# Group sizes, queue order and three seams of a streaming encoder layer on one Trainium2 core

## The chip, the core and the metric

The kernel is one program on one core of a Trainium2 chip. The metric is the device time of one execution in microseconds, as the median of several executions. The engines are called as in the profile: PE is TensorE (matrix products), DVE VectorE, ACT ScalarE, POOL GpSimd, and SP is the engine that here only issues DMA transfers.

## The reference

One layer on 512 prompt frames and 64 sample frames (576 columns, written HT halves of 256 + 32), model width 2048, all in float32:

```python
mod = silu(c) @ w_ada + b_ada                       # 2048 -> 6 x 2048
sh1, sc1, g1, sh2, sc2, g2 = split(mod, 6)
h = rmsnorm(x, norm1) * (1 + sc1) + sh1
proj = h @ w_in                                     # 2048 -> 7200 columns: q, k, v, gates of two head groups
...                                                 # gated linear attention (A), gated delta rule (B), per 64-frame block
x = x + g1 * (concat(o_a, o_b) @ w_out)             # 2048 -> 2048
h = rmsnorm(x, norm2) * (1 + sc2) + sh2
gate, val = split(h @ w_up, 2)                      # 2048 -> 2 x 5632
x = x + g2 * ((silu(conv3(gate) + b) * val) @ w_down)
y = rmsnorm(x, final_norm)
```

## The kernel before

**Products in three parts.** To reach float32 accuracy, every operand is split into a rounded part and a difference: weights `raw` into `wh` (ACT, rounding copy) and `wl = raw - wh` (DVE), activations into `hh` and `hl` in the same way. `mm6` multiplies one 128-row block of weights with one block of activations in six matmuls: `hh·wh`, `hl·wh`, `hh·wl`, each for the two halves of the columns. An engine works through its queue in order, so what is written ahead of an instruction on its engine is also executed ahead of it.

**First stage (`head`).** The modulation must be known before the first product, and its weights (`w_ada`) are as large as the projection's own. So the 16 blocks of 128 rows of x are taken in groups, `GROUPS` (first block, number of blocks). For each group `modulation(g)` runs eight steps (four 128-row chunks of `w_ada` each, out of `hraw` tiles), four for the scale `s1`, then four for the shift `mod`. After each four, the rows are copied from PSUM (`rw`, L864), transposed back to columns on PE (`bank<-consts,rw`), summed (`msum`, L869) and put into `mod` (L1006). Then `make(k)` forms a block's `hh` and `hl` through `split_mod`: scale and shift into `tmp` (L666 on ACT or L668 on DVE), rounding to `hh` (L669, ACT), difference `hl` (L670, DVE). While a group's products run for six early column tiles of `w_in` (`EARLY`, as three pairs, weights split in `pair_split`, L985 and L986, and partial sums kept by `sum_early` in `acc`), the next group's modulation steps are taken between the products: `product` steps the generator as a share of the products done. A narrow set of columns (`nar`, `ps_nar`) goes along with the first pair.

**In-projections.** The rest of `w_in` follows, with the recurrences of both head groups as jobs that a planner places between the matmuls by the costs in a table (their recorded line is L1978 on DVE and ACT, L1990 and L1994 on PE).

**Output projection.** `load_o` brings the heads' outputs of group B from DRAM and splits them. For each of 16 column tiles m, `x_tile(m)` loads the tile of x into one of two `xr` buffers and transposes it on PE (L1990 `bank<-consts,xr`, L1429), `gemm` multiplies, and `residual` adds.

**Up-projection.** For each step (t, c), a tile of columns and one of its seven products, `up_product` issues the matmuls (L1630 to L1632). Behind the first product, `norm_end` sums the squares over the partitions on PE (L1543), takes the power -1/2 on POOL (L1546), spreads the result into a diagonal `dg` (L1548, DVE) and broadcasts it over the partitions with PE again (L1554). The down-projection and the final norm follow.

Of the kernel before, what the change touches and what calls it, by code (L numbers as in the profile page):

```python
# [8 lines left out]
F32 = mybir.dt.float32  # L9
# [90 lines left out]
class Kern:  # L100
# [545 lines left out]

    def gemm(self, ps, src, acts, order=None, tick=lambda: None):

        n, i = len(acts), 0
        for k0 in order or range(0, n, 8):  # L650
            k1 = min(n, k0 + 8)
            wh, wl = self.wtile(src(k0, k1))
# [7 lines left out]

    def split_mod(self, x, s, b, hh, hl, tmp, other=False):

        nc = self.nc
        for c, q in ((slice(0, HP), 0), (slice(HP, HT), 1)):
            if other:
                nc.scalar.activation(tmp[:, :, c], x[:, :, c], AF.Identity, bias=b[:, q:q + 1], scale=s[:, q:q + 1])  # L666
                continue
            nc.vector.tensor_scalar(tmp[:, :, c], x[:, :, c], s[:, q:q + 1], b[:, q:q + 1], op0=ALU.mult, op1=ALU.add)  # L668
        nc.scalar.activation(hh, tmp, AF.Copy)  # L669
        nc.vector.tensor_tensor(hl, tmp, hh.bitcast(F32), op=ALU.subtract)  # L670

# [76 lines left out]
    def head(self, pool):  # L748
# [96 lines left out]
        def modulation(g):  # L845
            (m0, nm), per = GROUPS[g], per_tile(g)
            w = nm * P
            for n in range(8 * g, 8 * g + 8):
                _, mi, k0 = todo[n]
                ada_ahead(n + 1)  # L850
                if k0 == 0:
                    ps = self.bank()
                for k in (2, 3, 0, 1):
                    with self.tc.issue_after(last) if k == 0 else nullcontext():
                        T.matmul(ps[32 * k:32 * k + 32, :w], cs[:, k0 + k], got[n][k // per][:, k % per], start=(k0 == 0), stop=(k0 == KD - 4))  # L855
# [8 lines left out]
                V.tensor_copy(rw[:, :w], ps[:, :w])  # L864
# [4 lines left out]
                V.tensor_reduce(m, pc.rearrange("p b (j q) -> p b q j", j=4)[:, :, 0:2], axis=mybir.AxisListType.X, op=ALU.add)  # L869
# [7 lines left out]
        def w_ahead(n):  # L877
            for j in range(len(raws), min(n, len(pairs))):
                g, e = pairs[j]
                raws[j] = self.pair_load([off + h * P for _, off, h in EARLY[e:e + 2]], *GROUPS[g]), GROUPS[g][1]  # L880

        first, summed = modulation(0), []
# [12 lines left out]
        for b in range(5):  # L895
            if b < 4:
                x_norm(b + 1)
            if b < 3:
                x_square(b + 2)
            x_turn(b, (lambda b=b: x_scale(b + 1)) if b < 4 else None)  # L900
            if b > 0:
                next(first)
            if b == 3:
                v_turn(1)
        for _ in first:
# [6 lines left out]
        accs = [pool.tile([P, 2, HT], F32, tag=f"acc{e}", bufs=1, name=f"acc{e}") for e in range(len(EARLY))]  # L912

        def make(k):
            hh, hl = self.htiles(k)
            tmp = pool.tile([P, 2, HT], F32, tag="tmp", bufs=2, name=self.name("tmp"))
            self.split_mod(xT[:, k], s1[:, k], self.mod[:, 0, k], hh, hl, tmp, k in (1, 3))
            self.h.append((hh, hl))

        for g, (m0, nm) in enumerate(GROUPS):  # L920
# [6 lines left out]
            def product(e, j, k):  # L927
                nonlocal done, stepped
                self.mm6(ps[j], w[j][0][:, k - m0], w[j][1][:, k - m0], self.h[k], k == m0, k == ks[-1])
                done += 1  # L930
                while stepped < 10 and stepped * (units - nm) < 10 * done:
                    next(mods, None)
                    stepped += 1

            for e in range(0, len(EARLY), 2):
                w = self.pair_split(*raws[3 * g + e // 2])
                ps = [self.pgt() for _ in range(2)]
# [41 lines left out]

    def pair_split(self, raw, n):  # L980
# [3 lines left out]
        with self.tc.high_priority(offset=AHEAD):  # L984
            nc.scalar.activation(hi, raw[:, :2 * w], AF.Copy)  # L985
            nc.vector.tensor_tensor(lo, raw[:, :2 * w], hi.bitcast(F32), op=ALU.subtract)  # L986
        return [[x[:, e * w:(e + 1) * w].rearrange("p (k n) -> p k n", k=n) for x in (hi, lo)] for e in range(2)]
# [95 lines left out]

    def narrow_split(self, pool, src):

# [3 lines left out]
        nc.scalar.activation(s[:, :, 0:32], r, AF.Copy)  # L1089
        nc.vector.tensor_tensor(s[:, :, 32:64], r, s[:, :, 0:32].bitcast(F32), op=ALU.subtract)  # L1090
        return s
# [443 lines left out]
    def norm_end(self):  # L1535
# [6 lines left out]
        for b in range(5):  # L1542
# [5 lines left out]
        V.tensor_tensor(dg[:w], self.c["ident"][:w, :w].unsqueeze(1).to_broadcast([w, 5, w]),  # L1548
                        rs[:w, :5].unsqueeze(2).to_broadcast([w, 5, w]), op=ALU.mult)
        rb = self.rb = self.sq  # L1550
        dv = dg.rearrange("p b t -> p (b t)")
# [143 lines left out]
    def up(self):  # L1695
# [7 lines left out]
        for n, (t, c) in enumerate(steps):  # L1703
# [7 lines left out]
            if n == 0:  # L1711
                self.norm_end()

# [150 lines left out]
def layer_kernel(tc, i, o):  # L1864
    nc = tc.nc
    with ExitStack() as ctx:
# [15 lines left out]
        with ExitStack() as early:  # L1882
            K.wp = pool(early, "wp", "right", bufs=3)
            with ExitStack() as right:
# [9 lines left out]
                with ExitStack() as st:  # L1894
# [177 lines left out]
```

## Time and profile before

| | us |
|---|---|
| median of 3 executions | 2871.62 (2870.5 to 2878.71) |
| the profiled execution | 2873.51 |
| its span | 2871.4 |
| PE busy | 2809.1 (98%) |
| DVE busy | 2101.3 (73%) |
| ACT busy | 1189.0 (41%) |
| mean granted PE clock | 0.991 |
| PE busy in the first 200 us | 174.74 |
| PE busy from 1300 to 2780 us | 1480.0 |

The times inside the program are of the profiled execution and count from the start of its span; its own time is 2.1 us longer than the span. A row of the timeline has the start, the duration, the engine, the line of the code and the tiles (output<-inputs), and in brackets the time for which the engine had been idle before it and what released it. The granted clock is 1.00 at full speed and 0.50 where the throttle halves it. A matmul's recorded duration holds its run through the array, so successive ones overlap in the rows.

### The profile page before, as it was taken

The numbers are of one execution on the slowest core, as the hardware profiler recorded it, in microseconds if no ns is written. First come the engines' busy times: TensorE is split into PE (matmuls) and PEld (weight loads), VectorE is DVE, ScalarE is ACT, GpSimd is POOL, SyncE is SP. The second block draws the span as 40 slices with busy tenths as digits, with TensorE's granted clock in tenths as the row PEclk, the third lists the DMA queues.
The fourth block names the chain that finished last, engine by engine and source line by source line (L and its number), as shares of the span: only waits on it lengthen the run. The fifth ranks groups of instructions, "written<-read, shape, count | busy, mean of one in ns | idle before, by whom it ended". The sixth has DMA issues, their size and how long they took to land.

```text
span 2871.4 us, 52164 instructions
## 1 busy us (share of the span) xinstructions
PE 2809.1 (98%) x21028; PEld 2728.9 (95%) x21028; DVE 2101.3 (73%) x3592; ACT 1189.0 (41%) x2037; POOL 185.4 (6%) x244
## 2 busy tenths in 40 slices
PE   7999999999999999999999999999999999999998
PEld 4699999999999989999999999999999999999997
DVE  3478787787877888578888888888888855555565
ACT  4145555464534442454444444444444412212123
POOL 0001000010000000000111111111111000000000
PEclk8999999999999999999999999999999999999999
DMA  9965454455554567633333333333333653333221
GB/s 295 298 201 169 134 147 138 142 155 146 168 147 132 159 179 207 177 106 97 108 112 106 104 101 108 107 112 106 106 101 109 197 174 102 111 105 114 82 82 67
DMA packets 539797, 395.55 MB, mean 138 GB/s; under 512 B 59913, under 2 KB 477956, under 8 KB 539556
## 3 DMA queue, kind: packets, MB, share of 16 engines
q1 hardware_dynamic: 532212, 390.54, 45.8%
q8 instruction: 166, 2.72, 0.4%
q10 hardware_dynamic: 7344, 1.67, 0.3%
q14 instruction: 75, 0.61, 0.1%
HBM read 356.47 MB, written 35.67 MB: 137 GB/s over the span
## 4 chain that ended last, share of the span: by engine, by line
PE 86%; DVE 5%; issue 3%; DMA 3%; ACT 2%; POOL 1%; SPq 0%; ACTq 0%; POOLq 0%; DVEq 0%
PE g L643 29%; PE g L645 14%; PE bank L1631 12%; PE bank L1630 12%; PE bank L1632 11%; PE bank L1994 4%; DVE acc L1978 2%; PE bank L1990 1%; PE bank L855 1%; DVE wl L1978 1%; DVE m L1954 1%; DMA m<-gd 1%; DMA d<-m 1%; ACT m L1954 0%; DVE m L1978 0%
## 5 line engine op out<-in xcount | busy, mean ns | idle before, releaser
L1631 PE MATMUL bank<-slot,wh 128*128 128x290 f32 x2464 | 737.9, 299 | 0.0
L1630 PE MATMUL bank<-slot,wh 128*128 128x290 f32 x2464 | 734.2, 298 | 0.0
L1632 PE MATMUL bank<-slot,wl 128*128 128x290 f32 x2464 | 729.5, 296 | 0.0
L643 PE MATMUL g<-slot,wh 128*128 128x288 f32 x3168 | 550.4, 295 | 0.2 <-DVE slot L1978 0.2
L643 PE MATMUL g<-hh,wh 128*128 128x288 f32 x2048 | 475.2, 313 | 8.3 <-ACT hh L669 3.3
L1632 PEld LDWEIGHTS bank<-slot,wl 128*128 128x128 f32 x2464 | 471.4, 191 | 0.0
L1631 PEld LDWEIGHTS bank<-slot,wh 128*128 128x128 f32 x2464 | 468.8, 190 | 0.1
L1630 PEld LDWEIGHTS bank<-slot,wh 128*128 128x128 f32 x2464 | 463.8, 188 | 0.1
L643 PEld LDWEIGHTS g<-slot,wh 128*128 128x128 f32 x3168 | 463.0, 188 | 0.7 <-DVE slot L1978 0.5
L1978 ACT ACTIVATE wh<-raw 128x1024 fp32r<-128x1024 f32 x215 | 227.5, 1058 | 550.1 <-PE g L643 529.1
L643 PE MATMUL g<-hl,wh 128*128 128x288 f32 x2048 | 443.7, 298 | 0.0
L645 PE MATMUL g<-hh,wl 128*128 128x288 f32 x2048 | 441.9, 297 | 0.5 <-DVE wl L986 0.5
L1978 DVE SCALAR_TENSOR_TENSOR slot<-g,mod,slot 128x512 f32<-128x512 f32 (+1 forms) x448 | 201.8, 492 | 259.6 <-PE g L645 258.8
L643 PEld LDWEIGHTS g<-hh,wh 128*128 128x128 f32 x2048 | 327.0, 191 | 31.0 <-issue 16.3
L645 PE MATMUL g<-slot,wl 128*128 128x288 f32 x1584 | 340.9, 294 | 0.0
L643 PEld LDWEIGHTS g<-hl,wh 128*128 128x128 f32 x2048 | 331.9, 190 | 6.3 <-issue 5.4
L645 PEld LDWEIGHTS g<-hh,wl 128*128 128x128 f32 x2048 | 330.9, 189 | 6.1 <-issue 5.2
L1978 DVE TENSOR_TENSOR wl<-raw,wh 128x1024 fp32r<-128x1024 f32 x215 | 261.9, 1218 | 50.3 <-ACT wh L1978 47.9
L1577 ACT ACTIVATE wh<-raw 128x1024 fp32r<-128x1024 f32 x176 | 186.1, 1058 | 225.4 <-PE bank L1631 198.4
L645 PEld LDWEIGHTS g<-slot,wl 128*128 128x128 f32 x1584 | 255.3, 188 | 0.0
L1578 DVE TENSOR_TENSOR wl<-raw,wh 128x1024 fp32r<-128x1024 f32 x176 | 215.4, 1224 | 53.8 <-ACT wh L1577 53.8
L1577 ACT ACTIVATE wh<-s 128x1024 fp32r<-128x1024 f32 x132 | 140.1, 1062 | 210.7 <-DVE s L1588 109.3
(319 smaller groups left out, 3228.4 us busy)
## 6 DMA issues: line engine op xcount, KB each, us to landing
raw<-in_w_up_dram SPq DMA_DIRECT2D x176, 512.0 KB
raw<-in_w_in_dram SPq DMA_DIRECT2D x100, 512.0 KB
raw<-in_w_down_dram SPq DMA_DIRECT2D x88, 512.0 KB
aw<-in_w_ada_dram SPq DMA_DIRECT2D x79, 512.0 KB
xr<-in_w_ada_dram SPq DMA_DIRECT2D x49, 512.0 KB
hraw<-in_w_ada_dram SPq DMA_DIRECT2D x40, 512.0 KB
raw<-in_w_out_dram SPq DMA_DIRECT2D x32, 512.0 KB
slot<-actd SPq DMA_DIRECT2D x44, 288.0 KB
```

Of the source, the lines that this page charges most:

```text
L643: T.matmul(ps[:, h if bank is None else bank, :n], wh, x[:, h, :n], start=f, stop=False)
L645: T.matmul(ps[:, h if bank is None else bank, :n], wl, ah[:, h, :n], start=False, stop=stop)
L855: T.matmul(ps[32 * k:32 * k + 32, :w], cs[:, k0 + k], got[n][k // per][:, k % per], start=(k0 == 0), stop=(k0 == KD - 4))
L1577: self.nc.scalar.activation(hi, src, AF.Copy)
L1578: self.nc.vector.tensor_tensor(lo, src, hi.bitcast(F32), op=ALU.subtract)
L1630: T.matmul(ps, wh[:, j], hi, start=(c < 3 and j == 0), stop=False, skip_group_check=True)
L1631: T.matmul(ps, wh[:, j], lo, start=False, stop=False, skip_group_check=True)
L1632: T.matmul(ps, wl[:, j], hi, start=False, stop=(j == NPAIR - 1), skip_group_check=True)
L1954: return f(*a, **kw)
L1978: return f(*a, **kw)
L1990: return self.engine.transpose(out, *a)
L1994: return self.engine.matmul(out, *a, **kw)
```

## The change

In the first stage the 16 blocks are cut into six groups (2, 2, 3, 4, 3, 2) where there were five (2, 3, 4, 4, 3). `split_mod` is divided: `scale_x` multiplies x as soon as the scale is known, `shift_x` adds the shift while it rounds to `hh` (ACT, with a bias) and forms `hl` with one instruction per part (DVE). The first group's weight differences and the narrow difference are ordered behind the last row of the modulation (`issue_after`). After the copy of the rows, the modulation yields twice, and with a mark (`WAIT`) at which `product` stops stepping, so that products stand between the copy and the transposes; up to twelve steps are counted where there were ten. The vectors' transposes (`late`) are taken from any group behind the first.

Before the output projection the first weight tile is loaded and split after the fourth of eight `load_o`, and `x_tile(0)` comes behind the first tile's product. In the up-projection `norm_end` becomes a generator that stops after `dg`; its broadcast follows the second product.

```diff
-GROUPS = ((0, 2), (2, 3), (5, 4), (9, 4), (13, 3))
+GROUPS = ((0, 2), (2, 2), (4, 3), (7, 4), (11, 3), (14, 2))
...
-    def split_mod(self, x, s, b, hh, hl, tmp, other=False):
+    def scale_x(self, x, s, tmp, other=False):
         for c, q in ((slice(0, HP), 0), (slice(HP, HT), 1)):
             if other:
-                nc.scalar.activation(tmp[:, :, c], x[:, :, c], AF.Identity, bias=b[:, q:q + 1], scale=s[:, q:q + 1])
-                continue
-            nc.vector.tensor_scalar(tmp[:, :, c], x[:, :, c], s[:, q:q + 1], b[:, q:q + 1], op0=ALU.mult, op1=ALU.add)
-        nc.scalar.activation(hh, tmp, AF.Copy)
-        nc.vector.tensor_tensor(hl, tmp, hh.bitcast(F32), op=ALU.subtract)
+                nc.scalar.activation(tmp[:, :, c], x[:, :, c], AF.Copy, scale=s[:, q:q + 1])
+            else:
+                nc.vector.tensor_scalar_mul(tmp[:, :, c], x[:, :, c], s[:, q:q + 1])
+
+    def shift_x(self, b, hh, hl, tmp):
+        for c, q in parts:
+            nc.scalar.activation(hh[:, :, c], tmp[:, :, c], AF.Identity, bias=b[:, q:q + 1])
+        rounded = nc.cur_bb.bb.instructions[-1]
+        for c, q in parts:
+            nc.vector.scalar_tensor_tensor(hl[:, :, c], tmp[:, :, c], b[:, q:q + 1], hh[:, :, c].bitcast(F32),
+                                           op0=ALU.add, op1=ALU.subtract)
...
                 V.tensor_copy(rw[:, :w], ps[:, :w])
                 if g > 0:
-                    yield
+                    yield WAIT
+                    yield WAIT
...
+        for k in range(2):
+            scale(k)
         for _ in first:
             pass
-        nar = self.narrow_split(pool, nar)
+        summed_all = last()
+        begun = [self.pair_split(*raws[0], (None, summed_all))]
+        nar = self.narrow_split(pool, nar, summed_all)
+        for k in range(2):
+            make(k)
+        w_ahead(3)
+        begun += [self.pair_split(*raws[n], (rounded[-1], last())) for n in (1, 2)]
...
-                while stepped < 10 and stepped * (units - nm) < 10 * done:
-                    next(mods, None)
+                while stepped < 12 and (stepped - 2) * (units - nm - 2) < 10 * done:
+                    r = next(mods, None)
                     stepped += 1
+                    if stepped == 7 and not end:
+                        for i in range(2):
+                            scale(m0 + nm + i)
+                    if r is WAIT:
+                        break
...
-                        if g == 1 and e == 2 and late:
+                        if g > 0 and e == 2 and late:
                             late.pop(0)()
...
             self.up_product(t, c)
             if n == 0:
-                self.norm_end()
+                norm = self.norm_end()
+            if n < 2:
+                next(norm, None)
...
-                    ob = [K.load_o(k, lambda k=k: K.htiles(k)) for k in range(8, 16)]
+                    w, ob = {}, []
+                    for k in range(8, 16):
+                        ob.append(K.load_o(k, lambda k=k: K.htiles(k)))
+                        if k == 11:
+                            w[0] = K.wtile(K.w_cols("w_out", 0, 8)(0, 8))
...
-                        K.x1.append(K.x_tile(m))
-                        K.gemm(ps, K.w_cols("w_out", m, 8), ob, tick=K.tick)
+                        if m > 0:
+                            K.x1.append(K.x_tile(m))
+                        K.gemm(ps, K.w_cols("w_out", m, 8), ob, tick=K.tick, w=w.get(m))
+                        if m == 0:
+                            K.x1.append(K.x_tile(m))
```

On DVE at the entry to group 0, before, from the sum of the shift's rows on (`rw` are the copied rows, `wl` weight differences, `tmp` the scaled and shifted block, `nar` the narrow difference):

```order
L869 TENSOR_REDUCE msum_512<-bank_509 128x4
L986 TENSOR_TENSOR wl_619<-raw_355,wh_618 128x512
L1006 TENSOR_TENSOR mod<-msum_512,cols 128x4
L668 TENSOR_SCALAR tmp_534<-xT,s_218,mod 128x2x256
L668 TENSOR_SCALAR tmp_534<-xT,s_218,mod 128x2x32
L986 TENSOR_TENSOR wl_694<-raw_358,wh_693 128x512
L670 TENSOR_TENSOR hl_533<-tmp_534,hh_532 128x576
```

and the same place now:

```order
L880 TENSOR_REDUCE msum_521<-bank_518 128x4
L1043 TENSOR_TENSOR mod<-msum_521,cols 128x4
L1023 TENSOR_TENSOR wl_525<-raw_253,wh_524 128x512
L1128 TENSOR_TENSOR nar_528<-hraw_256,nar_528 128x2x32
L678 SCALAR_TENSOR_TENSOR hl_533<-tmp_489,mod,hh_532 128x2x256
L678 SCALAR_TENSOR_TENSOR hl_533<-tmp_489,mod,hh_532 128x2x32
```

`mod` has moved ahead of the weight difference, the scaling has left this place (it stands ahead of the copy of the rows), and two weight differences have moved behind `hl`, one ahead of it.

On PE at the entry to the second group, before, from the last modulation step of the shift to the first product of the new group (`bank_712` takes the transposes, `hh_736` is the new group's first block, `bank_786` the modulation of the group after it):

```order
L855 MATMUL bank_638<-hraw_608,cs 32x384 x2
L855 MATMUL bank_638<-hraw_607,cs 32x384 x2
L1990 MATMUL bank_712<-consts_185,rw_690 128x128 x3
L855 MATMUL bank_786<-hraw_644,cs 32x512 x2
L855 MATMUL bank_786<-hraw_643,cs 32x512
L643 MATMUL g_774<-hh_736,wh_770 128x288 x2
```

and now (`hh_728` is the new group's first block):

```order
L865 MATMUL bank_621<-hraw_511,cs 32x256 x4
L643 MATMUL g_696<-hh_538,wh_548 128x288 x2
L643 MATMUL g_696<-hl_539,wh_548 128x288 x2
L645 MATMUL g_696<-hh_538,wl_549 128x288
L2038 MATMUL bank_683<-consts_185,rw_668 128x128 x2
...
L643 MATMUL g_697<-hl_539,wh_548 128x288 x2
L645 MATMUL g_697<-hh_538,wl_549 128x288 x2
L865 MATMUL bank_776<-hraw_581,cs 32x384 x2
L865 MATMUL bank_776<-hraw_580,cs 32x384
L643 MATMUL g_764<-hh_728,wh_760 128x288 x2
```

Five matmuls of the running group now stand between the modulation step and the transposes, and thirteen more (the one left of `g_696` and the twelve of `g_697`) between these and the next group's modulation.

On PE at the start of the output projection, before (`g_11956` is the first column tile, `xr_11958` the first tile of x):

```order
L645 MATMUL g_11735<-hh_1111,wl_11822 128x288 x2
L643 MATMUL g_11956<-hh_11910,wh_11972 128x288
L1990 MATMUL bank_11962<-consts_185,xr_11958 128x128 x4
L1429 MATMUL bank_11968<-consts_185,xr_11958 128x64
L643 MATMUL g_11956<-hh_11910,wh_11972 128x288
```

and now the end of that column tile (`g_12081`) and the start of the second (`g_12173`):

```order
L645 MATMUL g_12081<-hh_12077,wl_12053 128x288 x2
L2038 MATMUL bank_12162<-consts_185,xr_12158 128x128 x4
L1467 MATMUL bank_12168<-consts_185,xr_12158 128x64
L643 MATMUL g_12173<-hh_12029,wh_12189 128x288 x2
L643 MATMUL g_12173<-hl_12030,wh_12189 128x288 x2
L2038 MATMUL bank_12179<-consts_185,xr_12175 128x128 x4
```

The transposes of x's first tile have moved from the first matmul of the column tile to behind its last, and those of the second tile follow after four matmuls of the second column tile.

More of the change, by code (lines that the diff above doesn't have):

```diff
@@ L645, in mm6, with gemm @@
             T.matmul(ps[:, h if bank is None else bank, :n], wl, ah[:, h, :n], start=False, stop=stop)
-    def gemm(self, ps, src, acts, order=None, tick=lambda: None):
+    def gemm(self, ps, src, acts, order=None, tick=lambda: None, w=None):
         n, i = len(acts), 0
@@ L651, in gemm @@
             k1 = min(n, k0 + 8)
[L652 removed]
+            wh, wl = w or self.wtile(src(k0, k1))
             for k in range(k0, k1):
@@ L880, in w_ahead, with scale, make @@
                 raws[j] = self.pair_load([off + h * P for _, off, h in EARLY[e:e + 2]], *GROUPS[g]), GROUPS[g][1]
+        scaled, rounded = {}, []
+        def scale(k):
+            if k not in scaled:
+                tmp = scaled[k] = pool.tile([P, 2, HT], F32, tag="tmp", bufs=2, name=self.name("tmp"))
+                self.scale_x(xT[:, k], s1[:, k], tmp, k in (1, 3))
+        def make(k):
+            hh, hl = self.htiles(k)
+            scale(k)
+            rounded.append(self.shift_x(self.mod[:, 0, k], hh, hl, scaled[k]))
+            self.h.append((hh, hl))
         first, summed = modulation(0), []
@@ L978, in pair_load, with after, pair_split @@
         return raw
-    def pair_split(self, raw, n):
+    def after(self, ins):
+        return self.tc.issue_after(ins) if ins is not None else nullcontext()
+    def pair_split(self, raw, n, order=None):
         nc, w = self.nc, n * P
         hi, lo = [self.wq.tile([P, 1024], F32R, tag="w" + c, bufs=3, name=self.name("w" + c))[:, :2 * w] for c in "hl"]
-        with self.tc.high_priority(offset=AHEAD):
-            nc.scalar.activation(hi, raw[:, :2 * w], AF.Copy)
-            nc.vector.tensor_tensor(lo, raw[:, :2 * w], hi.bitcast(F32), op=ALU.subtract)
+        act, dve = order or (None, None)
+        with self.tc.high_priority(offset=AHEAD) if order is None else nullcontext():
+            with self.after(act):
+                nc.scalar.activation(hi, raw[:, :2 * w], AF.Copy)
+            with self.after(dve):
+                nc.vector.tensor_tensor(lo, raw[:, :2 * w], hi.bitcast(F32), op=ALU.subtract)
         return [[x[:, e * w:(e + 1) * w].rearrange("p (k n) -> p k n", k=n) for x in (hi, lo)] for e in range(2)]
@@ L1089, in narrow_split @@
         nc.scalar.activation(s[:, :, 0:32], r, AF.Copy)
-        nc.vector.tensor_tensor(s[:, :, 32:64], r, s[:, :, 0:32].bitcast(F32), op=ALU.subtract)
+        with self.after(dve):
+            nc.vector.tensor_tensor(s[:, :, 32:64], r, s[:, :, 0:32].bitcast(F32), op=ALU.subtract)
         return s
@@ L1549, in norm_end @@
                         rs[:w, :5].unsqueeze(2).to_broadcast([w, 5, w]), op=ALU.mult)
+        yield
         rb = self.rb = self.sq
```

13 lines of the change are left out of this document (6 added, 7 removed).

## The prediction

> **What bounds the kernel now.** I read the profile's page first, then the windows by stage, then the timeline around every stop of TensorE. The page:
>
> ```profile
> span 2871.4 us, 52164 instructions
> PE 2809.1 (98%) x21028; PEld 2728.9 (95%) x21028; DVE 2101.3 (73%) x3592; ACT 1189.0 (41%) x2037; POOL 185.4 (6%) x244
> ```
>
> TensorE is busy for 2809.1 of 2871.4 us, so all its stops together are 62 us; nothing in the change lessens the products themselves. The windows of the first and the longest stage (length; then busy time and count of each engine; then granted clock, DMA share, GB/s) say where the stops are:
>
> ```profile
> 0.00:200.00 200.00, 174.74 (x1225) 129.51 (x1226) 99.06 (x223) 67.86 (x121) 5.18 (x16) 0.95 0.85 268
> 1300.00:2780.00 1480.00, 1480.00 (x11047) 1480.00 (x11046) 1089.35 (x1451) 558.00 (x657) 106.70 (x131) 1.00 0.38 113
> ```
>
> The up-projection (last row) has no stop at all, at 1480 / 11047 = 0.134 us a matmul. What can be won lies in the first 200 us (25.3 us idle, clock 0.95) and at two seams, near 1045 and 1288, whose rows stand below. All the edits of the change lie there.
>
> **First stage, entry to group 0.** The turn from modulation rows to the first product, in the timeline (start, duration, instruction, and in brackets the idle time before it and its releaser):
>
> ```profile
> 38.34 0.44 PE L1990 MATMUL bank<-consts,rw 128*128 128x128 f32 x2 [0.56 <-DVE rw L864]
> 38.82 0.17 DVE L869 TENSOR_REDUCE msum<-bank 128x4 f32<-128x16 f32 x1 [0.54 <-PE bank L1990]
> 38.93 0.69 DVE L986 TENSOR_TENSOR wl<-raw,wh 128x512 fp32r<-128x512 f32 x1
> 39.54 0.16 DVE L1006 TENSOR_TENSOR mod<-msum,cols 128x4 f32<-128x4 f32 x1
> 39.79 0.81 ACT L666 ACTIVATE tmp<-xT,mod,s 128x512 f32<-128x512 f32 x1 [1.69 <-DVE mod L1006]
> 40.54 0.68 ACT L669 ACTIVATE hh<-tmp 128x576 fp32r<-128x576 f32 x1
> 41.36 0.72 PE L1097 MATMUL ps_nar<-hh,nar 128*66 128x288 f32 x2 [2.58 <-ACT hh L669]
> ```
>
> The chain is msum, a weight difference that isn't needed yet (0.69), mod, scale and shift, rounding to hh, product: 2.58 us of TensorE. The change puts mod directly behind msum (saves 0.6) and scales ahead of the chain, so that one shift of 0.7 to 0.9 (256-column halves of the 0.68 row, and a second start) stands where tmp 0.81 and hh 0.68 stood (saves 0.7 to 0.9). The first product moves from 41.36 to about 39.85: **-1.5**. The weight difference, the narrow difference and hl now stand behind mod, but six matmuls that need only hh (0.8 us at full clock) cover them.
>
> What the pause does to the clock:
>
> ```profile
> 37.35:40.76 3.41, 0.88 (x10) 0.20 (x2) 2.33 (x7) 1.60 (x3) 0.00 (x0) 1.00 1.03 374
> 46.00:48.00 2.00, 2.00 (x7) 1.03 (x6) 0.00 (x0) 0.00 (x0) 0.00 (x0) 0.60 0.35 129
> 64.66:68.07 3.41, 1.35 (x10) 0.28 (x8) 1.95 (x6) 1.79 (x4) 0.00 (x0) 1.00 1.05 407
> 70.00:72.00 2.00, 2.00 (x8) 1.32 (x8) 0.90 (x2) 0.86 (x2) 0.00 (x0) 0.63 0.35 86
> ```
>
> After a 3.41-us stretch with 0.88 us of matmuls the clock is halved until about 47.6; after one with 1.35 us, until about 71.5. The first costs half of some 6.2 busy us, 3.1; the second half of 3.4, 1.7. With the products starting at 39.85 the first stretch would hold 0.88 + 0.91 = 1.79 of its 3.41 us, 52%. The trace halves at 40% and, after the pause of 1.25 at 102 (below), not at 63%; 52% lies between. I take half: **-1.6**, between 0 and -3.1. The Trainium skill ("TensorE: Matmul & The Clock Gate", HAM oscillation) says to avoid PE-idle gaps longer than about 3.4 us. By that rule none of the stops named in this text would touch the clock, every clock term would be zero, and the sum would come to -6.4 instead of -13.5. This trace contradicts it: the gaps here are 2.58 and 2.06 us and the clock was 0.50. The same page's fixed windows of about 3.4 us (Part 1) agree with the 3.41 us between the changes in the rows.
>
> **First stage, entry to the next group.**
>
> ```profile
> 64.46 0.55 PE L1990 MATMUL bank<-consts,rw 128*128 128x128 f32 x3 [0.71 <-DVE rw L864]
> 65.15 0.96 DVE L986 TENSOR_TENSOR wl<-raw,wh 128x768 fp32r<-128x768 f32 x1
> 68.06 0.85 PE L643 MATMUL g<-hh,wh 128*128 128x288 f32 x2 [2.06 <-ACT hh L669]
> ```
>
> In the changed order the transposes stand behind 5 or more matmuls (0.67 us for the 0.71), and 13 matmuls and three modulation matmuls (about 2.0 us) stand between them and the first matmul that needs hh. The difference wl still precedes mod here, but is 512 instead of 768 columns wide, and the scaling is done early: msum to hh takes 0.17 + 0.69 + 0.16 + 0.7 and hand-overs, about 2.0. So 0.7 and 1.6 us of idle go, and the 1.7 us of half clock: **-4.0**. Late next is hl, 0.4 us behind hh, which I keep of the 2.06.
>
> The other waits of the stage that the edits touch:
>
> ```profile
> 80.00 0.44 PE L1990 MATMUL bank<-consts,rw 128*128 128x128 f32 x2 [0.84 <-DVE rw L864]
> 83.83 0.53 PE L645 MATMUL g<-hh,wl 128*128 128x288 f32 x2 [0.53 <-DVE wl L986]
> 90.06 0.29 PE L712 MATMUL bank<-consts,hs 88*128 88x88 f32 x1 [0.77 <-DVE cols L713]
> 90.70 0.28 PE L712 MATMUL bank<-consts,hs 72*128 72x72 f32 x1 [0.34 <-DVE cols L713]
> 102.05 0.80 PE L643 MATMUL g<-hh,wh 128*128 128x288 f32 x4 [1.25 <-ACT hh L669]
> 112.90 0.44 PE L1990 MATMUL bank<-consts,rw 128*128 128x128 f32 x2 [0.39 <-DVE rw L864]
> ```
>
> They come to 4.1. In the changed order four later turns still have their transposes directly behind the last modulation matmul, for which I carry 0.7 each (the 0.71 row), and 0.4 for a late hl: 3.2 stay, **-0.9**.
>
> What six groups cost more than five is eight modulation steps:
>
> ```profile
> 62.90 0.85 PE L855 MATMUL bank<-hraw,cs 128*32 128x384 f32 x8
> 73.20 1.07 PE L855 MATMUL bank<-hraw,cs 128*32 128x512 f32 x8
> ```
>
> The columns stay the same in all, so only the fixed part is new: 128 columns are 1.07 - 0.85 = 0.22 us, which leaves 0.85 - 3 x 0.22 = 0.19 a step, some of it the last matmul's drain. Eight are 1.0 to 1.5, and up to 2.6 if what follows a step starts late too: **+1.6**. The six more partial sums run on VectorE and ScalarE, which are busy 99 and 68 of the 200 us: nothing while that holds, 0.7 each where a product would wait. ScalarE gets one more table load in the chain of the narrow columns at the stage's end; the one below takes 1.28, and the waits there are partly ScalarE's: 0 to 1.3, **+0.6**. The two 2-block groups also bring the modulation weights' deadlines closer (rival 2); the rows there leave a few us, so **+1.0**, 0 to 7.6. The stage: -1.5 - 1.6 - 4.0 - 0.9 + 1.6 + 0.6 + 1.0 = **-4.8**.
>
> **Seam before the output projection.**
>
> ```profile
> 1040.19 1.05 SPq L739 DMA_DIRECT2D raw<-in_w_out_dram  x2
> 1042.43 1.28 ACT L1978 ACT_TABLE_LOAD   x1
> 1045.88 1.06 ACT L1978 ACTIVATE wh<-raw 128x1024 fp32r<-128x1024 f32 x1 [1.28 <-DMA raw<-in_w_out_dram]
> 1046.99 0.40 PE L643 MATMUL g<-hh,wh 128*128 128x288 f32 x1 [3.03 <-ACT wh L1978]
> 1048.65 1.09 PE L1990 MATMUL bank<-consts,xr 128*128 128x128 f32 x4 [1.25 <-DMA xr<-in_x_prompt_dram]
> 1050.00:1052.00 2.00, 2.00 (x11) 2.00 (x10) 2.00 (x5) 0.48 (x2) 0.00 (x0) 0.50 0.89 244
> 1054.00:1056.00 2.00, 2.00 (x16) 2.00 (x15) 0.00 (x0) 0.00 (x0) 0.00 (x0) 0.87 1.00 310
> ```
>
> The first weight tile is asked for at 1040.19 and rounded at 1046.9: 3.03 us of waiting, then 1.25 for x, then half clock until about 1054.5 over 5.8 busy us, 2.9: 7.2 lost. Now the weights are asked for eight SP transfers earlier and split before the seam; x's transposes stand behind the 48 matmuls of column tile 0 (6.4 us). What is late next is the second x tile: its transposes follow the first products of tile 1, and its buffer comes free only when the last rows have been split, which now stand behind more ScalarE and VectorE work. That gives 0 to 5 us of new wait; I carry 2.2: **-5.0**.
>
> **Seam after the first up-projection product.**
>
> ```profile
> 1286.00 1.08 PE L1543 MATMUL bank<-consts,sqa 128*116 128x1 f32 x10
> 1288.96 0.76 DVE L1548 TENSOR_TENSOR dg<-consts,s 116x580 f32<-116x580 f32 x1 [1.31 <-POOL s L1546]
> 1289.78 2.08 PE L1554 MATMUL bank<-dg,consts 116*128 116x290 f32 x4 [2.69 <-DVE dg L1548]
> 1290.00:1292.00 2.00, 2.00 (x6) 1.42 (x6) 2.00 (x5) 0.85 (x3) 0.00 (x0) 0.51 0.09 23
> ```
>
> 2.69 idle and half of about 3.4 us at half clock, 4.4. The yield puts 24 matmuls (24 x 0.134 = 3.2 us) into the gap. VectorE is full in the window of the last row, and the products now ask for their split tiles 4 us earlier, so I count half as given back: **-2.2** (-4.4 to 0).
>
> **Inside the in-projections** the planner's turns shift:
>
> ```profile
> 275.19 1.10 PE L1994 MATMUL bank<-m,m 128*128 128x64 f32 x8 [2.78 <-DVE m L1978]
> ```
>
> These squarings of the inverse stand some 11 matmuls (1.5 us) later in the changed order: **-1.5** (-3 to +1).
>
> **Sum.** -4.8 - 5.0 - 2.2 - 1.5 = -13.5. The profiled execution took 2873.5 (span 2871.4 and 2.1 around it), 1.9 above the median of 2871.6; carried to the median the forecast is **2858.1**.
>
> **Rivals.**
> 1. *The first stage gives nothing.* The clock still halves (+1.6), the steps cost their upper end (+1.0) and a fifth group entry brings another 1.25 besides the waits at 80 to 113 returning (+0.9 and 1.25): -4.8 becomes 0. For it: the chain mod, shift, hl is repeated once more. Then 2871.6 - 8.7 = 2862.9, or a little over.
> 2. *Transfers take over: slower.*
>
> ```profile
> 60.00:70.00 10.00, 7.23 (x44) 3.24 (x43) 4.44 (x10) 4.33 (x7) 0.00 (x0) 0.90 1.04 376
> 80.00:90.00 10.00, 8.76 (x62) 7.17 (x62) 3.47 (x9) 0.85 (x1) 0.32 (x1) 1.00 1.05 352
> ```
>
>    A block's modulation and early weights are 2.5 MB. With groups of 2, 2, 3, 4 blocks, 17.5 MB are wanted between about 44 us, when the tiles are full, and the end of the third group near 98: 324 GB/s. Full windows gave 352 and 376, which is enough. It decides the other way below 324: at the stage's mean of 268 the weights come 11.3 us late, in some five pauses of over 2 us that each halve the clock for a stretch (1.7 each, 8.5). With the seams' -8.7 and the stage's other terms at about +0.5 that is +11.6: 2883. Smaller rows per transfer speak for it, the 350s against.
> 3. *The wait at 1045 only moves* to the second x tile or weight tile: its bound of 5 us and no clock gained there leave -2: 2861.1.
>
> **Chances.** Forecast 0.54, rival 1 0.20, rival 3 0.11, rival 2 0.15. About 0.3% (8.6 us) is what a measurement of this kernel tells from no change, so faster is below 2863.0 and slower above 2880.2. Of the forecast 0.48 are faster and 0.06 same; of rival 1 0.06 and 0.14; of rival 3 0.06 and 0.05; of rival 2 0.02 are same and 0.13 slower. Faster 0.60, same 0.27, slower 0.13. The range starts at 2848 (clock kept throughout, no new wait at the seams: -1.6, -2.2, -2.2, -1.5 and 2.5 more) and reaches to 2875, over rivals 1 and 3; it leaves out rival 2 and some 3% below.
>
> **What would show it.** Right: the first narrow product near 39.9 with under 1.3 us idle ahead of it; no half clock around 70; no pause above 1 us at the weights of the output projection, and its clock full; 24 matmuls of the next product between the column sums and the broadcast. Wrong: TensorE waiting for hraw or raw between 60 and 100 at under 324 GB/s (rival 2); four or more pauses above 1 us at group entries (rival 1); a stop of over 3 us about 7 us into the output projection (rival 3).

## The result, and the profile after

The changed kernel takes 2854.29 us (median of 4 runs, 2851.53 to 2856.73) against 2871.26 before (four executions): a ratio of 0.9935 (95% interval 0.9916 to 0.9954), 17 us less by the medians and 18.7 by the ratio, which is not the quotient of the two medians. Run again beside the experiments below it took 2853.67 against 2871.84, ratio 0.9943 (0.9929 to 0.9957). The forecast was 2858.1 in a range of 2848 to 2875. Its profiled execution took 2851.53. The first part of its page, and the windows that answer to those of before:

```profile
span 2849.8 us, 52385 instructions
PE 2796.4 (98%) x21092; PEld 2724.1 (96%) x21092; DVE 2109.3 (74%) x3625; ACT 1193.3 (42%) x2058; POOL 186.5 (7%) x245
```

```profile
0.00:200.00 200.00, 178.18 (x1369) 140.52 (x1370) 114.15 (x274) 79.72 (x153) 5.29 (x17) 0.99 0.87 277
37.40:40.80 3.40, 3.40 (x16) 2.89 (x20) 2.69 (x6) 1.78 (x4) 0.00 (x0) 0.50 1.00 332
40.00:60.00 20.00, 20.00 (x163) 13.38 (x166) 4.77 (x15) 7.26 (x15) 0.26 (x1) 0.98 0.94 325
66.00:70.00 4.00, 2.28 (x17) 2.04 (x16) 2.38 (x9) 0.00 (x0) 0.32 (x1) 1.00 1.05 372
1040.00:1060.00 20.00, 20.00 (x141) 16.48 (x140) 13.11 (x27) 7.07 (x18) 2.51 (x2) 1.00 0.83 237
1264.00:1274.00 10.00, 8.84 (x64) 8.29 (x63) 8.27 (x18) 7.39 (x17) 1.50 (x3) 1.00 0.49 135
```

TensorE's busy time fell by 12.7 us although it does 64 matmul records more. Most of the reason stands in the view of spans and clocks, before and then after:

```profile
core 0: 2871.4 us, clock 0.991
```

```profile
core 0: 2849.8 us, clock 0.996
```

A ledger can be made of these rows. Clock lost: 0.009 x 2871.4 = 25.8 us before, 0.004 x 2849.8 = 11.4 after, so 14.4 less. Idle: 2871.4 - 2809.1 = 62.3 before, 53.4 after, 8.9 less. What is left is work at full clock, 1.7 more. Together 21.6, the difference of the spans. (The clocks are given to 0.001, so the first and the last term are good to some 2 us. They also count halved time in which TensorE stood idle, at the program's end above all: over its busy time the halved stretches cost 20.8 and 6.3 us, again 14.5 apart.) Two thirds of the gain of these two executions is clock, not idle time.

Not all of that is the change's. Up to the last transposes ahead of group 0 both kernels issue the same 148 matmuls, and the profile of the kernel before had two halved stretches there, with 9.7 us of busy time; its transposes came 2.9 us later. The rows are the kernel before, the kernel before with the norm seam alone, which has the same first stage, and the changed kernel:

```profile
0.00:38.34 38.34, 22.81 (x148) 13.61 (x148) 18.24 (x53) 23.79 (x58) 3.82 (x12) 0.87 0.96 292
0.00:35.80 35.80, 20.92 (x148) 13.11 (x148) 18.22 (x53) 22.50 (x57) 3.82 (x12) 1.00 0.96 288
0.00:35.44 35.44, 20.50 (x148) 12.99 (x149) 18.07 (x53) 23.10 (x58) 3.78 (x12) 1.00 0.97 288
```

So 4.9 of the 14.5 stand ahead of the change. Another 1.9 lie in the in-projections, which no edit touches directly. At the changed places the clock gave 7.8 us (9.5 before, 1.7 after) and idle time 7.9.

The timeline at the changed places. Entry to group 0:

```profile
35.92 0.17 DVE L880 TENSOR_REDUCE msum<-bank 128x4 f32<-128x16 f32 x1 [0.53 <-PE bank L2038]
36.12 0.16 DVE L1043 TENSOR_TENSOR mod<-msum,cols 128x4 f32<-128x4 f32 x1
36.23 0.69 DVE L1023 TENSOR_TENSOR wl<-raw,wh 128x512 fp32r<-128x512 f32 x1
36.32 1.81 ACT L675 ACTIVATE hh<-tmp,mod 128x512 fp32r<-128x512 f32 x4 [0.75 <-DVE mod L1043]
37.38 0.69 PE L1135 MATMUL ps_nar<-hh,nar 128*66 128x288 f32 x2 [1.50 <-ACT hh L675]
59.97 0.63 ACT L1021 ACTIVATE wh<-raw 128x512 fp32r<-128x512 f32 x1 [2.02 <-DMA raw<-in_w_in_dram]
66.72 1.21 DVE L668 TENSOR_SCALAR tmp<-xT,s 128x512 f32<-128x512 f32 x4
67.84 0.68 DVE L1023 TENSOR_TENSOR wl<-raw,wh 128x512 fp32r<-128x512 f32 x1
68.58 0.53 PE L645 MATMUL g<-hh,wl 128*128 128x288 f32 x2 [1.72 <-DVE wl L1023]
```

`mod` follows `msum` directly, and the pause is 1.50 us instead of 2.58; one half-clock stretch of 3.4 us follows (second window) where there were 6.8. At the second entry, near 55, TensorE does not stop at all (third window: 20.00 of 20.00). The last rows are a new wait, in the second group's second pair of column tiles. The difference `wl` is late, but not for a transfer: its `raw` and `wh` were there from 60.60 on. It stands in VectorE's queue behind the sum for the third group's scale (from 66.10) and behind the early scaling (1.21), which the change put there.

The seam of the output projection, the norm, and the squarings inside the in-projections:

```profile
1037.67 0.60 PE L2038 MATMUL bank<-consts,xr 128*128 128x128 f32 x4
1038.78 0.24 PE L1467 MATMUL bank<-consts,xr 64*128 64x64 f32 x1 [0.51 <-DMA xr<-in_x_sample_dram]
1265.80 1.18 PE L1581 MATMUL bank<-consts,sqa 128*116 128x1 f32 x10
1270.15 1.14 PE L1593 MATMUL bank<-dg,consts 116*128 116x290 f32 x4
1272.73 0.40 PE L1669 MATMUL bank<-slot,wh 128*128 128x290 f32 x1 [1.17 <-ACT sqa L1594]
266.90 1.10 PE L2042 MATMUL bank<-m,m 128*128 128x64 f32 x8 [1.56 <-DVE m L2026]
```

Of 3.03 + 1.25 us at the output projection 0.51 is left, and the clock stays at 1.00. The broadcast of the norm starts without a wait; the next product waits 1.17 for its copy by ScalarE. The squarings wait 1.56 instead of 2.78 in this execution, but 3.83 in another profile of the same kernel (shown below, with the in-projections).

### The profile page after: what moved, and what is told of

It reads as the page before. It is cut to its first block, busy times and chain, and to the rows that moved or that the text cites. A ratio compares the mean times of both kernels' runs of the same rounds, so it can differ in the third digit from the quotient of the medians.

```text
span 2849.8 us, 52385 instructions
## 1 busy us (share of the span) xinstructions
PE 2796.4 (98%) x21092; PEld 2724.1 (96%) x21092; DVE 2109.3 (74%) x3625; ACT 1193.3 (42%) x2058; POOL 186.5 (7%) x245
## 4 chain that ended last, share of the span: by engine, by line
PE 84%; DVE 7%; issue 3%; DMA 3%; ACT 2%; POOL 1%; SPq 0%; ACTq 0%; DVEq 0%; POOLq 0%
PE g L643 28%; PE g L645 14%; PE bank L1670 12%; PE bank L1669 11%; PE bank L1671 11%; PE bank L2042 4%; DVE acc L2026 2%; PE bank L2038 1%; PE bank L865 1%; DVE wl L2026 1%; DVE m L2002 1%; DMA d<-m 0%; DMA hs<-in_x_prompt_dram 0%; DVE ca L2026 0%; DMA cm<-d 0%
```

## The experiments

All are compared with the kernel before on the same chip. Three chips were used, one for each group of four that ran together; on these the kernel before took 2873.09 (the parts alone and five groups), 2870.34 (eight groups, the weights without x, both with matmuls that nothing reads) and 2871.84 us (six groups, the queue order, the plain yield and the changed kernel again). The differences in us are worked out from the ratios; the medians alone would give up to 3 us more or less.

**The parts alone.** *First stage only*: the change without the hunks of the two seams; two of them are shown.

```diff
-                norm = self.norm_end()
-            if n < 2:
-                next(norm, None)
+                self.norm_end()
...
-                        if k == 11:
-                            w[0] = K.wtile(K.w_cols("w_out", 0, 8)(0, 8))
```

> The change's first-stage edits alone, both seams as before. Theory A (each part works at its own place, read from the two traces: lead of the changed kernel at the start of the output projection 13.4 us, of which 2.9 stood there before the first edited instruction): about -9 against before, 2862 us, first product under 1.6 us of idle behind the transposes, no halved clock around 65 to 72. Theory B (the stage gives nothing because the extra group's steps and waits eat it, and the lead is a chance of the clock at the start): 0 to -2, 2870 us.

2864.23 us, ratio 0.9974 (0.9966 to 0.9983): -7.5 us. A, a little less than its -9, and with a pause of 1.50 at the entry. Its other sign failed: the clock was halved at 66.93, behind the new wait of 1.72 us, which left the clock whole in both profiles of the changed kernel.

```profile
66.93:70.34 3.41, 3.41 (x19) 3.13 (x21) 0.76 (x1) 0.07 (x1) 0.00 (x0) 0.50 1.12 355
```

*Output seam only*: the kernel before with the hunks of `gemm` and `w[0]`, and `x_tile(0)` behind the product.

> The output projection's seam alone in the kernel before: first weight tile loaded and split early, first x tile behind the first product. Theory A: the seam's 4.3 us of idle and 2.9 us of half clock go, all but 0.5: -6.5, 2865 us, no pause above 1 us and the clock at 1.00 in the 20 us around the seam. Theory B (the wait moves to the second x tile, whose buffer comes free later): -2, 2869 us, with a pause of 2 to 5 us about 7 us into the output projection.

2862.71 us, ratio 0.9972 (0.9962 to 0.9981): -8.0. A. The only pause there is 0.69, for x:

```profile
1047.90 0.24 PE L1429 MATMUL bank<-consts,xr 64*128 64x64 f32 x1 [0.69 <-DMA xr<-in_x_sample_dram]
```

*Norm seam only*: the kernel before with the `yield` behind `dg` and the second `next`.

> Only the norm's broadcast moved behind the second up-projection product, in the kernel before. Theory A: the 2.69 us pause and the half clock (1.7) go and about 1.2 to 2.2 come back as a wait on the broadcast's copy and on VectorE: -2, 2869 us. Theory B (VectorE is full there, all is given back): 0, 2871 us, with TensorE waits of 2 us or more between 1290 and 1310.

2868.86 us, ratio 0.9988 (0.9979 to 0.9996): -3.4, interval -6.0 to -1.1. A, with the rest of the wait where it is in the changed kernel:

```profile
1293.21 0.40 PE L1631 MATMUL bank<-slot,wh 128*128 128x290 f32 x1 [1.14 <-ACT sqa L1556]
```

The three parts add to -18.9; the whole measured -18.7 (0.9935) and -16.4 (0.9943). Each part is good to 2 or 3 us, so this agrees, but it doesn't prove that the parts are independent.

**The weights without x.** The kernel before with `w[0]`, but `x_tile(0)` ahead of the product as before.

```diff
+                        if k == 11:
+                            w[0] = K.wtile(K.w_cols("w_out", 0, 8)(0, 8))
...
                         K.x1.append(K.x_tile(m))
-                        K.gemm(ps, K.w_cols("w_out", m, 8), ob, tick=K.tick)
+                        K.gemm(ps, K.w_cols("w_out", m, 8), ob, tick=K.tick, w=w.get(m))
```

> The kernel before with the output projection's first weight tile early, but x's first tile still transposed ahead of the first product. Theory A (x's transfer, asked for at 1042 and landed at 1048.5, is the wait behind the wait: TensorE then stops some 4 us for x and the clock still halves): 0 to -1.5 against before, 2872 us. Theory B (the weights alone make the stop): -6, 2867 us.

2867.45 us, ratio 0.9982 (0.9972 to 0.9993): -5.2. My reading (A) was wrong: x's transfer, asked for at 1045.49, came within 3.7 us, where it had taken 6.3, probably because the two large weight transfers were out of its way. TensorE waited 0.69 for it, and the clock was not halved:

```profile
1049.16 0.63 PE L1994 MATMUL bank<-consts,xr 128*128 128x128 f32 x4 [0.69 <-DMA xr<-in_x_prompt_dram]
```

What moving x as well is worth is not settled: 3 us by the ratios, but the intervals of -5.2 and -8.0 overlap, and in both traces one wait of 0.69 for x is left.

**The group sizes.** The change with five groups, with eight, and the kernel before with six.

```diff
-GROUPS = ((0, 2), (2, 2), (4, 3), (7, 4), (11, 3), (14, 2))
+GROUPS = ((0, 2), (2, 3), (5, 4), (9, 4), (13, 3))
```

> The whole change but with the old five groups (2, 3, 4, 4, 3). Theory A (the sixth group costs its eight steps, 1.5 us, and one more entry of about 0.8, and what it saves is no more than that): 2852 to 2855 us, within 2 us of the changed kernel. Theory B (the short second group is what lets the entry at 54 to 58 us pass without a pause): a pause of 1.5 us or more and a halved clock come back at the second entry, 2857 us or more.

2858.16 us, ratio 0.9957 (0.9945 to 0.9969): -12.4. The mechanism of B is there, a pause at the second entry with a halved clock behind it. The transposes stand directly behind 16 modulation matmuls again and wait 0.71 (at 58.79), in spite of the marks:

```profile
61.56 0.67 PE L643 MATMUL g<-hh,wh 128*128 128x288 f32 x3 [2.23 <-ACT hh L675]
60.00:70.00 10.00, 8.44 (x41) 4.35 (x42) 3.83 (x10) 3.81 (x8) 0.00 (x0) 0.83 0.83 269
```

The intervals of five and six groups overlap, so the 4 us between them are likely, not settled. The seams alone gave -8.0 and -3.4; of -12.4 that leaves some -1 for all edits of the first stage but the sizes (an estimate from three ratios, good to 5 us or so).

```diff
+GROUPS = tuple((n, 2) for n in range(0, 16, 2))
```

> The whole change with eight groups of two blocks. Theory A (a group costs its eight modulation steps at 0.19 us fixed and one entry of about 0.8): two more groups than six are +3.0 + 1.6, 2858 to 2861 us. Theory B (short groups starve on transfers, the prediction's rival 2): pauses above 1.5 us at hraw or raw between 60 and 150 us, 2865 us or more. Theory C (all entries get cheap, a pause below the clock's limit each): 2854 us or less.

2856.04 us, ratio 0.9943 (0.9930 to 0.9955): the same as six groups within the measurement. B is refuted: no pause at hraw or raw. A is not borne out either: 16 more steps, but behind the entry to group 0 no pause above 0.69 us up to 200 us and no halved clock. That is the mechanism of C, 2 us above its bound:

```profile
36.00:200.00 164.00, 156.99 (x1351) 130.79 (x1352) 105.37 (x252) 56.85 (x106) 1.72 (x7) 1.00 0.86 272
152.17 0.53 PE L643 MATMUL g<-hh,wh 128*128 128x288 f32 x2 [0.69 <-ACT wh L1021]
```

In the kernel before, six groups need one more edit, since the vectors' turns no longer fit into the second group:

```diff
+GROUPS = ((0, 2), (2, 2), (4, 3), (7, 4), (11, 3), (14, 2))
...
-                        if g == 1 and e == 2 and late:
+                        if g > 0 and e == 2 and late:
```

> The kernel before with the six groups alone (and the vectors' turns taken from any later group), scaling, queue order and yields as before. Theory A (small groups help only where the entry is short): the 2.6 and 2.1 us pauses with their halved clock stay, eight more steps: +1 to +2, 2873 us. Theory B (the group sizes alone carry the stage's gain): -3 to -5, 2867 us.

2865.90 us, ratio 0.9986 (0.9977 to 0.9995): -4.0, so B. The modulation's smaller tiles arrive early enough that a step of the next group now runs inside the entry pause, and cuts it into 1.05 and 0.89. At the second entry the old code now has its transposes among products, without a wait (third row), and neither the 0.71 nor the 2.06 of before comes back:

```profile
36.18 0.63 PE L855 MATMUL bank<-hraw,cs 128*32 128x256 f32 x6 [1.05 <-DMA hraw<-in_w_ada_dram]
37.70 0.45 PE L1097 MATMUL ps_nar<-hh,nar 128*66 128x288 f32 x2 [0.89 <-ACT hh L669]
52.23 0.38 PE L1990 MATMUL bank<-consts,rw 128*128 128x128 f32 x2
36.00:80.00 44.00, 39.95 (x311) 26.71 (x312) 18.48 (x44) 12.47 (x21) 0.58 (x2) 1.00 0.96 326
```

**The queue order and the marks.** The change with the differences ahead of the modulation again:

```diff
-        begun = [self.pair_split(*raws[0], (None, summed_all))]
-        nar = self.narrow_split(pool, nar, summed_all)
+        begun = [self.pair_split(*raws[0])]
+        nar = self.narrow_split(pool, nar)
...
-        begun += [self.pair_split(*raws[n], (rounded[-1], last())) for n in (1, 2)]
```

> The whole change, but at the entry to the first group the weight differences and the narrow difference stand again where the scheduler puts them, ahead of the modulation. Theory A (the chain msum, difference, mod is 0.6 to 0.7 longer, and the pause of about 2.1 us halves the clock more often): +1 to +3 against the changed kernel, 2856 us. Theory B (the difference is hidden by scaling done ahead): within 1 us of it.

2857.51 us, ratio 0.9957 (0.9944 to 0.9969), 3.8 us above the changed kernel's 2853.67 on the same chip, with overlapping intervals. The pause is 2.05 as in A. A second one grew that A did not name: the differences now stand ahead of the copy of the rows too, and the transposes wait 1.86 where they waited 0.55:

```profile
35.69 0.44 PE L2037 MATMUL bank<-consts,rw 128*128 128x128 f32 x2 [1.86 <-DVE rw L874]
38.18 0.72 PE L1134 MATMUL ps_nar<-hh,nar 128*66 128x288 f32 x2 [2.05 <-ACT hh L675]
```

The change with a plain yield behind the copy:

```diff
-                    yield WAIT
-                    yield WAIT
+                    yield
```

> The whole change, but with one plain yield where the modulation waits twice with a mark, so the transposes come directly behind the copy of the rows more often. Theory A (about 0.7 us of TensorE idle comes back at each place where products stood between, five of eleven): +2 to +4 against the changed kernel, 2857 us. Theory B (other waits there end later anyway): within 1 us.

2851.84 us, ratio 0.9938 (0.9926 to 0.9951), against 2853.67 (0.9943): B, no difference beyond the intervals. Nothing here shows a use of the double mark.

**The clock alone.** Matmuls that nothing reads, in a pause of the kernel before; all other work is kept.

```diff
                         ps = K.pgt()
+                        if m == 0:
+                            junk = K.bank()
+                            for _ in range(20):
+                                K.nc.tensor.matmul(junk[:, :288], ob[0][0][:, 0, :P], ob[0][0][:, 0, :288], start=True, stop=True)
```

> The kernel before with 20 matmuls (2.7 us) into a bank that nothing reads, in the pause ahead of the output projection; both waits stay as they are, the results too. Theory A (the clock halves for want of work in a fixed 3.41-us stretch, and that costs half of what runs until it is back): clock 1.00 behind the pause, -2.5 to -3, 2870 us, although TensorE has more to do. Theory B (only the idle time counts): 0 or slower.

2870.15 us, ratio 0.9992 (0.9981 to 1.0003): inconclusive. The matmuls ran, but x's transposes had moved ahead of the first product, TensorE then stopped 2.05 us for x, and the clock still halved, for one stretch instead of two:

```profile
1041.85 2.80 PE L1912 MATMUL bank<-hh 128*128 128x288 f32 x20
1046.70 0.63 PE L1994 MATMUL bank<-consts,xr 128*128 128x128 f32 x4 [2.05 <-DMA xr<-in_x_prompt_dram]
```

At the entry to group 0:

```diff
         for _ in first:
             pass
+        jb = self.bank()
+        for _ in range(15):
+            T.matmul(jb[:, :HP], self.c["ident"], xT[:, 0, 0, :HP], start=True, stop=True)
```

> The kernel before with 15 matmuls (about 2.4 us) that nothing reads in the pause between the transposes and the first product. Theory A (clock): no halved stretch at about 38 to 45 us where before had one of 6.83 us; the first product stays 2.6 us behind the transposes; -1.5 to -3, 2870 us. Theory B (only the wait counts): 0, 2873 us.

2864.78 us, ratio 0.9978 (0.9968 to 0.9989): -6.3, interval -9.2 to -3.2. The matmuls took 6.64 us, not 2.4, so the first product came 6.56 us behind the transposes instead of 3.02, and the kernel was still faster:

```profile
37.80 6.64 PE L909 MATMUL bank<-xT,consts 128*128 128x256 f32 x30
44.09 0.61 PE L1100 MATMUL ps_nar<-hh,nar 128*66 128x288 f32 x2
44.00:54.00 10.00, 10.00 (x84) 6.36 (x82) 0.79 (x3) 1.30 (x2) 0.32 (x1) 1.00 0.80 257
60.00:70.00 10.00, 10.00 (x68) 6.88 (x65) 5.32 (x11) 4.48 (x8) 0.00 (x0) 1.00 0.95 349
```

B's 0 is refuted, but the run alone does not isolate the clock: the order of the first products changed too, and the second entry, with its transfers 3.5 us ahead, no longer stopped (last row). By waits alone that makes +3.5 at the entry and -2.8 at the second. From the transposes to the last early product it took 139.98 us in the profile where the kernel before had 142.73, while the halved clock there cost 1.7 us in place of 4.8.

Five profiles side by side isolate the clock. Their kernels have the first stage of the kernel before, unchanged. From the last transposes ahead of group 0 to the end of the last early product (here the kernel before, the output seam only, and the weights without x):

```profile
38.34:181.07 142.73, 133.00 (x933) 97.19 (x934) 65.21 (x123) 30.99 (x45) 1.36 (x4) 0.96 0.82 264
34.39:174.43 140.04, 130.32 (x933) 96.79 (x934) 65.17 (x123) 31.87 (x47) 1.36 (x4) 0.99 0.84 273
36.67:180.54 143.87, 134.15 (x933) 98.26 (x934) 65.16 (x123) 31.98 (x47) 1.36 (x4) 0.95 0.83 266
```

The matmuls are the same 933 and the idle time is 9.7 us in each, yet the times lie 3.8 us apart. The clock records hold 9.6, 3.4 and 12.0 us of busy time at half clock. Half of that taken off leaves 137.9, 138.3 and 137.9 (the other two: 137.9 and 138.1). So with all waits alike a halved stretch costs half of its busy time, as the prediction priced it, and whether the same 2.58 us pause at the entry halves the clock for two stretches, for one or not at all differed between these profiles.

## Why the prediction was right

The sum was -13.5; -17.0 was measured. The price of a pause (its length, and half of the busy time in the halved stretches behind it) held, and so did the mechanism of both seams. In the first stage the gain came in part from elsewhere than I had it; idle time and costs were both put too high there and stood against each other, so that its total came out nearer than its terms, which is luck.

- **First stage, -4.8; alone -7.5 (-9.8 to -4.9).** The stretch from the last transposes ahead of group 0 to the last early product shows the terms, in the changed kernel, with five groups, and with six groups alone:

```profile
35.44:170.69 135.25, 128.37 (x997) 98.43 (x998) 72.73 (x156) 35.67 (x66) 1.52 (x5) 0.99 0.86 280
35.95:175.47 139.52, 129.56 (x933) 97.00 (x934) 66.87 (x139) 35.16 (x63) 1.67 (x4) 0.96 0.85 271
34.69:172.89 138.20, 130.92 (x997) 97.37 (x998) 71.05 (x140) 32.25 (x50) 1.51 (x5) 1.00 0.84 271
```

| | length | idle | halved clock | the rest |
|---|---|---|---|---|
| first stage as before, mean of 5 profiles | 142.36 | 9.73 | 4.35 (1.7 to 6.0) | 128.28 |
| the changed first stage (two profiles of the changed kernel and the one of the stage alone agree to 0.1) | 135.25 | 6.88 | 1.71 | 126.66 |
| the change with five groups | 139.52 | 9.96 | 5.12 | 124.44 |
| six groups alone | 138.20 | 7.28 | 0 | 130.92 |

  The stage gained 7.1 us: 2.9 of idle time where I had 4.7, 2.6 of clock where I had 3.3, and 1.6 in the rest, where I had a cost of 3.2. The chain at the entry is shorter by 1.08 us of pause, not 1.5: `mod` directly behind `msum` saved its 0.6, but the shift saved 0.5 and not 0.7 to 0.9. The second entry lost its 0.71, its 2.06 and its half clock (-4.0 as worked out), and four entries keep 0.7 to 0.84 each. Against that stands the wait of 1.72 at 68.6, for which I had no term. The idle time goes for the most part with the group sizes (7.3 with six groups alone) and not with the new order (10.0 with five groups), while I gave the sizes only a cost. Their eight steps do cost about what I said: 2.2 between five and six groups in the change, of 1.0 to 2.6. That the other edits took 3.8 off the rest I had not foreseen, and its cause stays open. At the entry to group 0 I counted the halved clock as all or nothing; both profiles of the changed kernel show one stretch (1.7 us), where the old first stage showed two stretches in three profiles, one in one and none in one. The +1.0 for transfers did not come: the stretch from 44 to 98 us, for which rival 2 wanted 324 GB/s, moved 335, and TensorE waited for no `hraw` or `raw` there.
- **Output seam, -5.0; alone -8.0 (-10.9 to -5.5).** The mechanism was right; the 2.2 us carried for a wait at the second x tile were too much. It did not come; 0.51 us is left, and at the sample rows of the first x tile.
- **Norm seam, -2.2; alone -3.4 (-6.0 to -1.1).** Half of 4.4 was given back in my sum. What comes back is 1.17 for ScalarE's copy of the broadcast and 0.20 for VectorE: of 4.4 about 3.0 is gained in the traces.
- **In-projections, -1.5.** Not shown. The pause of 2.78 is 1.56, but in the second profile of the changed kernel it is 3.83, the next large one, at 659 before, went from 1.97 to 2.54, and half-clock stretches in this part come and go between executions of one program.

```profile
267.78 1.97 PE L2042 MATMUL bank<-m,m 128*128 128x64 f32 x8 [3.83 <-DVE m L2026]
```

- **Rivals.** The first (the stage gives nothing) and the third (the wait only moves) are refuted by the parts alone, the second (transfers) by the changed kernel itself and by eight groups, where nothing waited for `hraw` or `raw`.
- **Signs.** No half clock came around 70, no pause above 1 us at the output projection, and the 24 matmuls stand where they should. The first sign failed: 1.50 us of idle ahead of the first narrow product, not under 1.3. That it ran at 37.38 and not near 39.9 is mostly the start: this execution was 2.9 us ahead at the transposes.

The part of the gain that is chance shows in the second profile of the same changed kernel (its span and clock, and the busy times of its page):

```profile
core 0: 2855.9 us, clock 0.994
```

```profile
PE 2801.5 (98%) x21092; PEld 2728.3 (96%) x21092; DVE 2109.2 (74%) x3625; ACT 1192.6 (42%) x2058; POOL 187.1 (7%) x245
```

It is 6.1 us longer with 1.0 us more idle time (2855.9 - 2801.5 = 54.4); nearly all the rest is clock, in the in-projections. The 22.0 us between the two profiled executions hold some 5 us of such luck beside the 17 of the medians; 2.9 of it stood there at the transposes ahead of group 0.

## What to carry to other kernels

On an engine whose clock depends on its recent work, price a pause twice: its own length, and half of what runs in the stretch after it if the pause takes the stretch around it to about half idle. So a pause that can't be removed is worth splitting in two or filling with work that is due later, and smaller pieces can win by this though they add instructions: six groups alone gave -4.0. When several edits go in together, take each out by itself before crediting it: here the group sizes, priced as a cost, took away most of the waits that the new order was credited with. And read what a late instruction waits for in the queue of its own engine: its inputs may have been there for long. Before believing a difference of 0.2%, look at the granted clock of each execution: here it went with most of the spread of one program.

## What the runs showed of the hardware

- **Which stretches halve the clock.** From the clock records and the matmul records of all 14 profiles, in stretches of 3.41 us between 20 us and the last 30: of 73 full-clock stretches that a halved one followed, 70 had TensorE busy for 56% or less (the other three 67, 67 and 84%); of the 11,335 that none followed, not one was under 46%. So about half a stretch of work decides, and a pause of 1.5 us can go either way by where it lies on the grid. The Trainium skill ("TensorE: Matmul & The Clock Gate", HAM oscillation) gives gaps of about 3.4 us as the limit; these runs contradict it, with pauses of 1.5 to 2.7 us. At the entry to group 0 the clock halved in both profiles of the changed kernel and not in those of eight groups, of the plain yield and of the first stage alone, with the same pause of 1.50 or 1.51.
- **What a thousandth of mean clock costs.** In the executions of the kernel before that ran beside the experiments, the span's median falls from 2874.7 us at a granted clock of 0.990 (4 executions) to 2864.2 at 0.994 (6), some 2.6 us a thousandth; in all 66 executions span and clock go together (correlation -0.81), so this is the larger part of one program's spread.
- **What a halved stretch costs.** Half of its busy time, with the same work and the same waits: 142.73 us less 4.8, 140.04 less 1.7 and 143.87 less 6.0 agree to 0.5 us.
